# Hybrid decoder block: the mixers' low weight parts, head halves and attention sums made by DMAs in place of vector instructions

## The chip, the cores and the metric

The kernel runs on one NeuronCore of a Trainium2 chip. The metric is the device time of one execution in microseconds, given as the median of several runs. A core has a matrix engine (TensorE, PE in the profile, with its weight loads as PEld), a vector engine (VectorE, DVE), an activation engine (ScalarE, ACT), a general engine (GpSimd, POOL) and a queue engine (SyncE, SP). Each runs its own list of instructions strictly in order; semaphores hold an instruction back until what it needs is there, and everything behind it on that engine waits too. DMAs are issued from SP (the "hardware" queue of the profile) and from POOL (the "software" queue); a DMA that adds to its destination is issued from POOL here.

## The reference

One layer of a hybrid trunk on 1024 tokens of width 1024, all in float32. What matters for the change is attention group B; the rest is cut.

```python
hn = rms_norm(h, norm1_g[i]);  proj = hn @ w_in[i]
a_b, a_c, a_h, q, k, v, c_u, c_v = jnp.split(proj, split_idx, axis=-1)
y_a = a_b * short_conv(a_c * a_h, conv_w[i])                 # width 256
q = rms_norm(q.reshape(bsz, s_len, 8, 64), q_norm_g[i]);  k = ...  # per head
# stick breaking, 8 heads of 64, strictly causal:
z = einsum(q, k) / 8
weights = where(causal, exp(log_sigmoid(z) + suffix_sum(log_sigmoid(-z))), 0)
y_b = einsum(weights, v)
y_c = spatial_gating(gelu(c_u), gelu(c_v), ...)              # width 256
h = h + concat([y_a, y_b, y_c]) @ w_out
f = square(relu(rms_norm(h, norm2_g) @ w_ff1));  h = h + f @ w_ff2
h = h + sigmoid(rms_norm(h, norm3_g) @ w_ple_gate) * (p @ w_ple_proj)
```

## The kernel before, in words

Nearly every product is made of three matmuls on numbers that are split into a rounded high part and a low remainder (`hi`, `lo`; float32r): hi·hi, hi·lo and lo·hi (`product`, L157). A split is two instructions: ACT writes `hi` (a rounding copy), then DVE, or POOL where `low` says so, writes `lo = x - hi` (`split`, L131). A weight tile comes by a DMA on SP into one of 7 staging buffers (`stage`, L64) and is split into two of 20 buffers of the pool `wp` (`load_w`, L141). The staging buffer is free again when `lo` is made; a pair of `wp` buffers is free when its last matmul has run.

Stages: loads and gating MLP (to about 80 us), then projection of the first pair of heads; then from about 105 to 412 us the attention of the four pairs of heads, each woven by `weave` (L262) with filling work for PE: the projection of the next pair (`project`, L306), and for the last pair the convolution's projections (`convolve`, L559); then `w_out`, the MLP (a Strassen-like scheme, 570 to 1172 us) and the gate.

`project(pr)` loads eight weight tiles of 128x384, one for each block of 128 input channels (`wk`, k = 0 to 7). For each of eight token blocks t it runs 24 matmuls (8 k times 3) into one of two PSUM banks, normalizes queries and keys (ACT square, DVE sums, POOL `rs` = power -1/2, DVE `qk`), and splits the values `V`. Every second t, `turn_qk` transposes `qk` on PE and splits it. Each token half (th = 0 for t = 0 to 3, th = 1 for t = 4 to 7) has tiles of 128x512 per head hh: `QS[hh]` stacks the high and the low part of the query on the two halves of the partitions, `KH[hh]` holds the key's high part twice, `KL[hh]` its low part once and zeros. Before, KL is written by two DVE instructions on 64 rows each (L370), the halves are brought to their places by three ACT copies (L374 to L376) and three DVE copies (L377 to L379) of 64x512.

`attend(pr)` goes through eight steps (head 0 with g = 0 to 3, then head 1 with g = 3 to 0; g is a block of 256 queries). `stick` makes `z` on PE, two sigmoids on ACT (`rem`, `wt`), a running product on DVE (L413), and a multiplication on POOL or DVE (L416). `gather` transposes the weights on PE (`w_tr`), splits them (ACT `wT_hi`, DVE `wT_lo`) and multiplies by V into `av`, whose two halves of partitions hold V's high and low contribution. Before, ACT copies the lower half out (L462) and DVE adds the upper (L463) into `y_b`, which goes to DRAM on SP.

Between the steps, `block_sums` (L282) issues DMAs on POOL that work on the MLP's second weight in DRAM (`w_sums`): at most two per call, of 1 MB each, plain (L300) or accumulating (L297), placed behind POOL's last multiplication of the step. The order on each engine is not that of the code alone: a scheduler places each instruction by a simulated timeline. A DMA on POOL also waits for the one eight DMAs earlier on that queue to have landed, and a DMA on SP likewise.

Of the kernel before, what the change touches and what calls it, by code (L numbers as in the profile page):

```python
# [32 lines left out]
def hybrid_block(ctx: ExitStack, tc: tile.TileContext, a: dict):  # L33
# [27 lines left out]
    def slot(s, dt=F32, shape=(P, HT)):  # L61
        return sp.tile(list(shape), dt, tag="slot", name=name(s))
# [10 lines left out]
    def halves(s, dt=F32, shape=(P, HT)):  # L73
        return [slot(s, dt, shape) for _ in range(2)]
# [4 lines left out]
    def half_tmp(s, dt=F32):  # L79
        return tp.tile([P, 256], dt, tag="half", name=name(s), bufs=3)  # L80
# [50 lines left out]
    def split(src, hi, lo, scale=None, low=nc.vector):  # L131

        if scale is None:
            nc.scalar.copy(hi, src)  # L134
            low.tensor_tensor(out=lo, in0=src, in1=hi, op=ALU.subtract)  # L135
        else:
            nc.scalar.activation(hi, src, AF.Copy, scale=scale)
            nc.vector.scalar_tensor_tensor(out=lo, in0=src, scalar=scale, in1=hi,  # L138
                                           op0=ALU.mult, op1=ALU.subtract)

    def load_w(src, cols, low=nc.vector):  # L141

        st = stage(src, cols)
        hi = wp.tile([P, 384], F32R, tag="w", name=name("whi"))
        lo = wp.tile([P, 384], F32R, tag="w", name=name("wlo"))
        split(st, hi[:, :cols], lo[:, :cols], low=low)
        return hi, lo

    def load_units(src):
# [155 lines left out]

    def project(pr):  # L306

        wk = [load_w(a["w_qkv"][pr, k], 384, nc.gpsimd if pr and k % 2 == 0 else nc.vector)
              for k in range(KT)]

        QS = [[None, None], [None, None]]

        KH = [[None, None], [None, None]]
        KL = [[None, None], [None, None]]
        V = [None] * 4
        low_q = [None, None]
        heads[pr] = QS, KH, KL, V, low_q
        for t in range(KT):
            th, ts = block(t)
            if t % 4 == 0:  # L320
                for hh, other in enumerate((hi_p, lo_p)):
                    KL[hh][th] = slot("KL", F32R)
                    nc.gpsimd.memset(KL[hh][th][other].bitcast(F32), 0.0)
                KH[0][th] = slot("KH", F32R)
                QS[0][th] = slot("QS", F32R)
                low_q[th] = slot("q_lo", F32R)
                QS[1][th] = slot("QS", F32R)
# [17 lines left out]
            nc.vector.tensor_tensor(  # L345
                out=qk[:, t % 2].rearrange("p (h d) -> p h d", d=HD),
                in0=ps[:, :256].rearrange("p (h d) -> p h d", d=HD),
                in1=rs.unsqueeze(2).broadcast_to([P, 4, HD]), op=ALU.mult)
            if t % 2 == 0:
                V[t // 2] = slot("V", F32R, (P, 2, 2, 2, HD))  # L350
            v = V[t // 2][:, t % 2]
            split(ps[:, 256:].rearrange("p (h d) -> p h d", d=HD), v[:, :, 0], v[:, :, 1], scale=r1[t])
            if t % 2 == 1:
                later(72, lambda t=t, qk=qk: turn_qk(heads[pr], t, qk))

    def turn_qk(head, t, qk):

        QS, KH, KL, _, low_q = head
        th = t // 4
        tr = bank(ps_tr, "qk_tr")  # L360
        for i in range(2):
            for j in range(2):
                o = j * 256 + i * P
                nc.tensor.transpose(tr[:, o:o + P], qk[:, i, j * P:(j + 1) * P], ident)
# [3 lines left out]
        nc.scalar.activation(KH[0][th][:, ws], tr[:, 256:], AF.Copy, scale=gk)  # L368
        for hh, own in enumerate((lo_p, hi_p)):
            nc.vector.scalar_tensor_tensor(out=KL[hh][th][own, ws], in0=tr[own, 256:],  # L370
                                           scalar=gk[own], in1=KH[0][th][own, ws],
                                           op0=ALU.mult, op1=ALU.subtract)
        if t % 4 == 3:
            nc.scalar.copy(KH[1][th][hi_p], KH[0][th][hi_p])  # L374
            nc.scalar.copy(KH[1][th][lo_p], KH[0][th][hi_p])
            nc.scalar.copy(KH[0][th][hi_p], KH[0][th][lo_p])  # L376
            nc.vector.tensor_copy(QS[1][th][hi_p], QS[0][th][hi_p])  # L377
            nc.vector.tensor_copy(QS[1][th][lo_p], low_q[th][hi_p])
            nc.vector.tensor_copy(QS[0][th][hi_p], low_q[th][lo_p])  # L379
        return 8  # L380

    PROJECT = KT * 72 + 32

    def attend(pr):

        QS, KH, KL, V, _ = heads[pr]
        yb = halves("y_b")
        weights = {}

        def stick(hh, g):  # L390
# [32 lines left out]
        def gather(hh, g):  # L423
# [21 lines left out]
            for j in range(-2, g + 1):  # L445
# [6 lines left out]
                for kb, o, first in parts:  # L452
                    m = 256 - first * P
                    lhs = V[kb // 2][:, kb % 2, hh].rearrange("p two d -> p (two d)")
                    for part in (hi, lo):
# [2 lines left out]
                                         stop=kb == 2 * g + 1 and part is lo)  # L458
                yield 8

            low = half_tmp("av_lo")
            nc.scalar.copy(low[:HD], av[HD:])  # L462
            nc.vector.tensor_tensor(out=yb[g // 2][own, (g % 2) * 256:(g % 2 + 1) * 256],  # L463
                                    in0=av[:HD], in1=low[:HD], op=ALU.add)
            if hh == 1 and g % 2 == 0:
                nc.sync.dma_start(y_dram[pr, g // 2], yb[g // 2])

        steps = [(0, g) for g in range(4)] + [(1, g) for g in reversed(range(4))]
        yield from stick(*steps[0])
# [127 lines left out]
    for h in range(2):  # L597
        for k in range(2):
            st = stage(a["pT"][k * P:(k + 1) * P, half[h]])
            if h == 0:  # L600
                wple.append([load_w(a["w_ple_proj"][k * P:(k + 1) * P, :384], 384)])
            p_parts[k][h] = pair("p")
            split(st, *p_parts[k][h])
    for c0, n in UNITS[1:]:
        for k in range(2):
            wple[k].append(load_w(a["w_ple_proj"][k * P:(k + 1) * P, c0 * P:(c0 + n) * P], n * P))
    vu_parts = []
    first_half = normalize(0)
    for n in range(KT):
# [475 lines left out]
```

## Time and profile before

| what | value |
|---|---|
| time, median of 3 runs | 1270.49 us (1269.83 to 1271.85) |
| the profiled execution's own time | 1269.84 us |
| its span | 1268.1 us |
| mean granted TensorE clock | 0.981 |
| PE / DVE / ACT / POOL busy | 1212.7 / 879.3 / 604.4 / 363.9 us |
| DMA packets, bytes | 118699, 234.89 MB |

A row of the profile's groups reads: line, engine, operation, out<-in, shapes, count | busy time, mean of one in ns | idle time of that engine just before, and what ended it. The view of windows gives, for each stretch of the span, the busy time of each engine with its number of instructions, and the granted clock of TensorE (1.00 is full speed). The view of waits names who waited for whom, with total, number and longest in us. Rows of DMA issues give count, size and the median time from issue to landing.

### The profile page before, as it was taken

The numbers are of one execution on the slowest core, as the hardware profiler recorded it, in microseconds if no ns is written. First come the engines' busy times: TensorE is split into PE (matmuls) and PEld (weight loads), VectorE is DVE, ScalarE is ACT, GpSimd is POOL, SyncE is SP. The second block draws the span as 40 slices with busy tenths as digits, with TensorE's granted clock in tenths as the row PEclk, the third lists the DMA queues.
The fourth block names the chain that finished last, engine by engine and source line by source line (L and its number), as shares of the span: only waits on it lengthen the run. The fifth ranks groups of instructions, "written<-read, shape, count | busy, mean of one in ns | idle before, by whom it ended". The sixth has DMA issues, their size and how long they took to land.

```text
span 1268.1 us, 17511 instructions
## 1 busy us (share of the span) xinstructions
PE 1212.7 (96%) x5868; PEld 1033.1 (81%) x5868; DVE 879.3 (69%) x1324; ACT 604.4 (48%) x1167; POOL 363.9 (29%) x365
## 2 busy tenths in 40 slices
PE   9999898899999898959999999999999999999998
PEld 7898798888888787748888888888888888888887
DVE  7746887898879654666877867777756465686443
ACT  7625655666566354553343333345644354555211
POOL 2324443465222212233543443431000000122110
PEclk9998998999999999979999999999999999999999
DMA  9503157788541287789999999858956565553231
GB/s 321 196 18 132 68 166 231 168 193 159 119 98 34 95 274 195 197 227 214 260 255 258 238 248 260 241 183 308 359 179 224 187 211 183 192 174 101 78 113 50
DMA packets 118699, 234.89 MB, mean 185 GB/s; under 512 B 13104, under 2 KB 20528, under 8 KB 118352
## 3 DMA queue, kind: packets, MB, share of 16 engines
q1 hardware_dynamic: 94752, 168.08, 39.5%
q0 software_dynamic: 23856, 65.70, 23.1%
q8 instruction: 46, 0.75, 0.3%
q14 instruction: 45, 0.37, 0.1%
HBM read 176.57 MB, written 78.64 MB: 201 GB/s over the span
## 4 chain that ended last, share of the span: by engine, by line
PE 82%; DVE 8%; DMA 5%; issue 2%; ACT 1%; POOL 0%; SPq 0%; DVEq 0%; POOLq 0%; ACTq 0%
PE d_ps L731 24%; PE f_ps L731 23%; PE qkv_ps L161 3%; PE qkv_ps L162 3%; PE qkv_ps L163 3%; PE g_ps L161 2%; PE g_ps L163 2%; PE g_ps L162 2%; DVE rem L413 2%; PE av L456 2%; DMA h_dram<-h 1%; PE w_tr L438 1%; PE cv_ps L161 1%; PE cv_ps L163 1%; PE cv_ps L162 1%
## 5 line engine op out<-in xcount | busy, mean ns | idle before, releaser
L135 DVE TENSOR_TENSOR w_lo<-raw,w_hi 128x512 fp32r<-128x512 f32 x268 | 238.9, 894 | 97.2 <-ACT w_hi L134 92.7
L134 ACT CAST w_hi<-raw 128x512 fp32r<-128x512 f32 x268 | 164.8, 619 | 246.1 <-PE d_ps L731 118.1
L731 PE MATMUL f_ps<-hn_hi,w_hi 128*128 128x512 f32 x448 | 176.4, 394 | 11.1 <-ACT v L872 11.1
L731 PE MATMUL f_ps<-hn_lo,w_hi 128*128 128x512 f32 x448 | 175.5, 392 | 0.0
L731 PE MATMUL f_ps<-hn_hi,w_lo 128*128 128x512 f32 x448 | 175.1, 391 | 0.0
L731 PE MATMUL d_ps<-f_hi,w_hi 128*128 128x512 f32 x448 | 174.3, 389 | 0.0
L731 PE MATMUL d_ps<-f_lo,w_hi 128*128 128x512 f32 x448 | 174.3, 389 | 0.0
L731 PE MATMUL d_ps<-f_hi,w_lo 128*128 128x512 f32 x448 | 174.3, 389 | 0.0
L731 PEld LDWEIGHTS f_ps<-hn_hi,w_hi 128*128 128x128 f32 x448 | 84.9, 190 | 29.5 <-ACT v L872 11.5
L719 POOL TENSOR_TENSOR S<-S,sq 128x512 f32<-128x512 f32 x14 | 22.2, 1588 | 274.3 <-ACT sq L785 274.3
L731 PEld LDWEIGHTS f_ps<-hn_lo,w_hi 128*128 128x128 f32 x448 | 84.8, 189 | 18.2 <-issue 0.5
L731 PEld LDWEIGHTS f_ps<-hn_hi,w_lo 128*128 128x128 f32 x448 | 84.8, 189 | 17.7
L731 PEld LDWEIGHTS d_ps<-f_hi,w_hi 128*128 128x128 f32 x448 | 84.1, 188 | 17.6
L731 PEld LDWEIGHTS d_ps<-f_hi,w_lo 128*128 128x128 f32 x448 | 84.1, 188 | 17.5
L731 PEld LDWEIGHTS d_ps<-f_lo,w_hi 128*128 128x128 f32 x448 | 84.1, 188 | 17.3
L413 DVE TENSOR_TENSOR_SCAN rem<-rem 128x128 f32<-128x128 f32 (+3 forms) x64 | 88.9, 1392 | 10.3 <-ACT rem L409 9.7
L161 PE MATMUL qkv_ps<-whi,xn_hi 128*128 128x384 f32 x256 | 91.8, 359 | 2.5 <-DVE V L138 2.5
L163 PE MATMUL qkv_ps<-whi,xn_lo 128*128 128x384 f32 x256 | 89.7, 351 | 0.0
L162 PE MATMUL qkv_ps<-wlo,xn_hi 128*128 128x384 f32 x256 | 89.4, 349 | 0.0
L135 DVE TENSOR_TENSOR f_lo<-raw,f_hi 128x512 fp32r<-128x512 f32 x112 | 77.5, 723 | 3.9 <-ACT f_hi L134 3.7
L416 POOL TENSOR_TENSOR wt<-wt,rem 128x127 f32<-128x127 f32 (+4 forms) x40 | 44.3, 1109 | 106.8 <-DVE rem L413 44.0
L134 ACT CAST f_hi<-raw 128x512 fp32r<-128x512 f32 x112 | 67.0, 620 | 16.2 <-DMA raw<-f_dram 12.1
(213 smaller groups left out, 2663.4 us busy)
## 6 DMA issues: line engine op xcount, KB each, us to landing
raw<-in_w_ff SPq DMA_DIRECT2D x160, 256.0 KB, 3.8
raw<-f_dram SPq DMA_DIRECT2D x112, 256.0 KB, 4.7
raw<-w_sums SPq DMA_DIRECT2D x64, 256.0 KB, 3.7
f_dram<-f SPq DMA_DIRECT2D x48, 256.0 KB, 4.2
f_dram<-t SPq DMA_DIRECT2D x48, 256.0 KB, 4.0
w_sums<-in_w_ff POOLq DMA_DIRECT2D x8, 1024.0 KB, 11.7
w_sums<-w_sums POOLq DMA_DIRECT2D x8, 1024.0 KB, 12.6
raw<-in_w_ff POOLq DMA_DIRECT2D x32, 256.0 KB, 5.2
```

The lines of the kernel that those rows point to most:

```text
L134: nc.scalar.copy(hi, src)
L135: low.tensor_tensor(out=lo, in0=src, in1=hi, op=ALU.subtract)
L161: nc.tensor.matmul(ps, lh, rh, start=first and i == 0, stop=False)
L162: nc.tensor.matmul(ps, lh, rl, start=False, stop=False)
L163: nc.tensor.matmul(ps, ll, rh, start=False, stop=last and i == len(terms) - 1)
L413: nc.vector.tensor_tensor_scan(out=back, data0=back, data1=back, initial=1.0, op0=ALU.mult, op1=ALU.bypass)
L416: done = (nc.vector if on_vector else nc.gpsimd).tensor_tensor(out=wt[:, :W - 1], in0=wt[:, :W - 1], in1=rem[:, 1:W], op=ALU.mult)
L438: nc.tensor.transpose(tr[:, n:n + P], wts[i][:, kb * P:(kb + 1) * P], ident)
L456: nc.tensor.matmul(av[:, first * P:], lhs, part[:, o:o + m], start=kb == 0 and part is hi, stop=kb == 2 * g + 1 and part is lo)
L719: return eng.tensor_tensor(out=out, in0=x, in1=y, op=ALU.add)
L731: nc.tensor.matmul(bank, l, r, start=first and k == 0 and i == 0, stop=k == len(b) - 1 and i == 2, skip_group_check=True)
```

## The change

Three edits, all in the mixers. (1) `load_w`, for the projections of `project` and `convolve` (50 tiles): ACT writes minus the rounded weight into `lo`, then `hi`; a DMA on POOL adds the weight itself to `lo`. The subtraction on DVE or POOL goes. The six tiles of `w_ple_proj` keep the old way. (2) `turn_qk`: the key's low part is made for all 128 rows by one DVE instruction into a tile of its own, `k_lo`; at the end of each token half eight DMAs of 64x512 on SP bring the halves of QS, KH and KL to their places. The six copies and one of two L370 go. The last two of the eight overwrite rows that earlier ones read, and so wait for those to have landed. (3) `gather`: ACT copies all 128 rows of `av` into a tile `av_sb` of one token half; after its second part an accumulating DMA on POOL adds the lower rows to the upper, and a DMA on SP stores 64 rows to DRAM (16 of each kind in place of 8 stores). ACT's copy of 64 rows and DVE's addition go.

```diff
-    def load_w(src, cols, low=nc.vector):
+    def load_w(src, cols, by_dma=True):
         st = stage(src, cols)
         hi = wp.tile([P, 384], F32R, tag="w", name=name("whi"))
         lo = wp.tile([P, 384], F32R, tag="w", name=name("wlo"))
-        split(st, hi[:, :cols], lo[:, :cols], low=low)
+        if by_dma:
+            nc.scalar.activation(lo[:, :cols], st, AF.Copy, scale=-1.0)
+            nc.scalar.copy(hi[:, :cols], st)
+            nc.gpsimd.dma_start(lo[:, :cols], st, accum_op=ALU.add)
+        else:
+            split(st, hi[:, :cols], lo[:, :cols])
         return hi, lo
...
-        wk = [load_w(a["w_qkv"][pr, k], 384, nc.gpsimd if pr and k % 2 == 0 else nc.vector)
-              for k in range(KT)]
+        wk = [load_w(a["w_qkv"][pr, k], 384) for k in range(KT)]
...
         split(tr[:, :256], QS[0][th][:, ws], low_q[th][:, ws], scale=gq)
-        nc.scalar.activation(KH[0][th][:, ws], tr[:, 256:], AF.Copy, scale=gk)
-        for hh, own in enumerate((lo_p, hi_p)):
-            nc.vector.scalar_tensor_tensor(out=KL[hh][th][own, ws], in0=tr[own, 256:],
-                                           scalar=gk[own], in1=KH[0][th][own, ws],
-                                           op0=ALU.mult, op1=ALU.subtract)
+        split(tr[:, 256:], KH[0][th][:, ws], low_k[th][:, ws], scale=gk)
         if t % 4 == 3:
-            nc.scalar.copy(KH[1][th][hi_p], KH[0][th][hi_p])
-            nc.scalar.copy(KH[1][th][lo_p], KH[0][th][hi_p])
-            nc.scalar.copy(KH[0][th][hi_p], KH[0][th][lo_p])
-            nc.vector.tensor_copy(QS[1][th][hi_p], QS[0][th][hi_p])
-            nc.vector.tensor_copy(QS[1][th][lo_p], low_q[th][hi_p])
-            nc.vector.tensor_copy(QS[0][th][hi_p], low_q[th][lo_p])
+            for to, src, rows, of in (
+                    (KH[1], KH[0], lo_p, hi_p), (KH[1], KH[0], hi_p, hi_p),
+                    (QS[1], QS[0], hi_p, hi_p), (QS[1], low_q, lo_p, hi_p),
+                    (KL[0], low_k, lo_p, lo_p), (KL[1], low_k, hi_p, hi_p),
+                    (KH[0], KH[0], hi_p, lo_p), (QS[0], low_q, hi_p, lo_p)):
+                nc.sync.dma_start(to[th][rows].bitcast(F32), src[th][of].bitcast(F32))
...
-            low = half_tmp("av_lo")
-            nc.scalar.copy(low[:HD], av[HD:])
-            nc.vector.tensor_tensor(out=yb[g // 2][own, (g % 2) * 256:(g % 2 + 1) * 256],
-                                    in0=av[:HD], in1=low[:HD], op=ALU.add)
-            if hh == 1 and g % 2 == 0:
-                nc.sync.dma_start(y_dram[pr, g // 2], yb[g // 2])
+            th = g // 2
+            first = (hh, th) not in sums
+            if first:
+                sums[hh, th] = slot("av_sb")
+            y = sums[hh, th]
+            nc.scalar.copy(y[:, (g % 2) * 256:(g % 2 + 1) * 256], av)
+            if not first:
+                nc.gpsimd.dma_start(y[:HD], y[HD:], accum_op=ALU.add)
+                nc.sync.dma_start(y_dram[pr, th][own], y[:HD])
+                del sums[hh, th]
```

The scheduler orders the mixers anew. Three places show it, all at the end of the second pair's attention, where the fourth pair's weights come in. Numbers in names are tile numbers and differ between the two programs: wt_3046 before is wt_3061 after, wlo_3167 is the low part of the last weight tile (k = 7) of the fourth pair, wlo_4044 and wlo_4051 belong to the convolution.

POOL before, around the four accumulating `w_sums` DMAs of that place:

```order
L416 TENSOR_TENSOR wt_3046<-wt_3046,rem_3045 128x255
L297 DMA w_sums<-in_w_ff 512x512 x2
L297 DMA w_sums<-w_sums 512x512 x2
L135 TENSOR_TENSOR wlo_3115<-stage_3112,whi_3114 128x384
L323 MEMSET KL_3148 64x512
L323 MEMSET KL_3150 64x512
L135 TENSOR_TENSOR wlo_3127<-stage_3124,whi_3126 128x384
L135 TENSOR_TENSOR wlo_3139<-stage_3136,whi_3138 128x384
L416 TENSOR_TENSOR wt_3214<-wt_3214,rem_3213 128x127
```

POOL after, at the same place (the last row is the accumulating DMA of the attention's sums of the second pair, head 1):

```order
L418 TENSOR_TENSOR wt_3051<-wt_3051,rem_3050 128x127
L150 DMA wlo_3160<-stage_3157 128x384
L418 TENSOR_TENSOR wt_3061<-wt_3061,rem_3060 128x255
L303 DMA w_sums<-in_w_ff 512x512 x2
L303 DMA w_sums<-w_sums 512x512 x2
L150 DMA wlo_3167<-stage_3164 128x384
L150 DMA wlo_4044<-stage_4041 128x384
L150 DMA wlo_4051<-stage_4048 128x384
L175 TENSOR_TENSOR rs_3110<-ss_3107,mhalf 128x4
L470 DMA av_sb_2939<-av_sb_2939 64x512
```

The weights' low parts were instructions of POOL and DVE; now three of them, and a sum, are DMAs that stand behind four 1 MB DMAs on the same queue. One pair earlier the same stands once: wt_2154, two accumulating `w_sums` DMAs, then wlo_2259 (the third pair's k = 4), av_sb_2032, wlo_2266.

SP after, a little later; each load waits for its staging buffer (stage_4445 for wlo_3167's DMA, stage_4452 for wlo_4044's), each store for its accumulating DMA, and the next two rows are the last joins for the third pair's second token half:

```order
L66 DMA stage_4445<-in_w_conv 128x384
L66 DMA stage_4452<-in_w_conv 128x384
L471 DMA y_dram<-av_sb_2939 64x512
L471 DMA y_dram<-av_sb_3192 64x512
L381 DMA KH_2703<-KH_2703 64x512
L381 DMA QS_2704<-q_lo_2705 64x512
```

Before, there were no joins on SP; its queue held loads and eight stores of `y_b` alone.

PE after, where these are used (z_3327 is the third pair's first score of t = 4, head 0):

```order
L168 MATMUL qkv_ps_3181<-wlo_3167,xn_hi_426 128x384
L169 MATMUL qkv_ps_3181<-whi_3166,xn_lo_427 128x384
L168 MATMUL qkv_ps_3298<-wlo_3167,xn_hi_426 128x384
L169 MATMUL qkv_ps_3298<-whi_3166,xn_lo_427 128x384
L458 MATMUL av_87<-wT_hi_3309,V_2402 128x256
L458 MATMUL av_87<-wT_lo_3310,V_2402 128x256
L458 MATMUL av_87<-wT_hi_3309,V_2402 128x128
L458 MATMUL av_87<-wT_lo_3310,V_2402 128x128
L404 MATMUL z_3327<-KH_2703,QS_2704 128x128
```

The scheduler has moved the k = 7 products of the first two token blocks (qkv_ps_3181, qkv_ps_3298) behind the rest of both; before, they stood with the others of their block, in the order of k. Both PSUM banks of the projection stay taken until they have run.

More of the change, by code (lines that the diff above doesn't have):

```diff
@@ L315, in project @@
         V = [None] * 4
-        low_q = [None, None]
-        heads[pr] = QS, KH, KL, V, low_q
+        low_q, low_k = [None, None], [None, None]
+        heads[pr] = QS, KH, KL, V, low_q, low_k
         for t in range(KT):
@@ L326, in project @@
                 low_q[th] = slot("q_lo", F32R)
+                low_k[th] = slot("k_lo", F32R)
                 QS[1][th] = slot("QS", F32R)
@@ L356, in turn_qk @@
     def turn_qk(head, t, qk):
-        QS, KH, KL, _, low_q = head
+        QS, KH, KL, _, low_q, low_k = head
         th = t // 4
@@ L384, in attend @@
     def attend(pr):
-        QS, KH, KL, V, _ = heads[pr]
-        yb = halves("y_b")
+        QS, KH, KL, V, *_ = heads[pr]
+        sums = {}
         weights = {}
@@ L600, in hybrid_block @@
             if h == 0:
-                wple.append([load_w(a["w_ple_proj"][k * P:(k + 1) * P, :384], 384)])
+                wple.append([load_w(a["w_ple_proj"][k * P:(k + 1) * P, :384], 384, False)])
             p_parts[k][h] = pair("p")
@@ L605, in hybrid_block @@
         for k in range(2):
-            wple[k].append(load_w(a["w_ple_proj"][k * P:(k + 1) * P, c0 * P:(c0 + n) * P], n * P))
+            wple[k].append(load_w(a["w_ple_proj"][k * P:(k + 1) * P, c0 * P:(c0 + n) * P], n * P, False))
     vu_parts = []
```

## The prediction

> **What bounds the kernel now.** I read the page first, then windows, then the waits of one stage.
>
> ```profile
> span 1268.1 us, 17511 instructions
> ...
> PE 1212.7 (96%) x5868; PEld 1033.1 (81%) x5868; DVE 879.3 (69%) x1324; ACT 604.4 (48%) x1167; POOL 363.9 (29%) x365
> ```
>
> PE is busy for 96% of the span, so an edit gains only where PE is idle or slow. The change touches the mixers; the windows cut at the starts of the pairs' attention (the first two numbers are the stretch and PE's busy time, then PEld, DVE, ACT, POOL, the granted clock and the DMA share).
>
> ```profile
> 112.00:190.00 78.00, 68.63 (x409) 64.60 (x409) 62.41 (x104) 46.49 (x111) 37.32 (x38) 0.93 0.44 141
> 190.00:268.00 78.00, 70.38 (x429) 66.37 (x429) 63.52 (x107) 48.31 (x118) 36.64 (x40) 0.93 0.69 191
> 268.00:340.00 72.00, 65.63 (x429) 61.86 (x429) 64.72 (x109) 48.04 (x116) 31.43 (x29) 1.00 0.77 152
> 340.00:442.00 102.00, 98.18 (x530) 83.11 (x529) 78.94 (x113) 52.98 (x115) 28.75 (x24) 1.00 0.34 83
> 442.00:460.00 18.00, 16.90 (x63) 13.75 (x64) 9.32 (x15) 8.67 (x16) 2.10 (x3) 0.81 0.84 282
> ```
>
> In the first four PE is idle for 9.4, 7.6, 6.4 and 3.8 us, 27 us in all. The clock of 0.93 in two windows of 78 us costs at most another 11 us. So 38 us is all that the mixers can give. DVE is busy for 269.6 of these 330 us (82%), and it is DVE that PE waits for, as the waits of PE from 90 to 435 us say (total us, times, longest):
>
> ```profile
> PE qk_tr L364 <- DVE qk L345: 5.5, 4, 2.7
> PE av L456 <- DVE wT_lo L135: 4.0, 4, 1.7
> PE w_tr L438 <- DVE wt L416: 3.1, 3, 1.4
> PE w_tr L438 <- DVE KL L370: 2.8, 2, 1.4
> PE av L456 <- DVE y_b L463: 2.7, 4, 1.3
> PE qkv_ps L161 <- DVE V L138: 2.5, 3, 0.8
> PE w_tr L438 <- DVE wT_lo L135: 2.2, 1, 2.2
> ```
>
> These are 22.8 us. No row names a DMA: weights reach PE through DVE in time.
>
> **The change part by part: what leaves.** The groups of the same stretch:
>
> ```profile
> L135 DVE TENSOR_TENSOR wlo<-stage,whi 128x384 fp32r<-128x384 f32 (+1 forms) x29 | 20.2, 708 | 6.9 <-ACT whi L134 6.8
> L134 ACT CAST whi<-stage 128x384 fp32r<-128x384 f32 (+1 forms) x40 | 18.9, 502 | 12.2 <-DMA stage<-in_w_qkv 6.1 <-PE cv_ps L162 5.0 <-DMA stage<-in_w_conv 0.8
> L370 DVE SCALAR_TENSOR_TENSOR KL<-qk_tr,c_gk,KH 64x256 fp32r<-64x256 f32 x32 | 15.3, 478 | 2.5 <-ACT KH L368 2.2
> L135 POOL TENSOR_TENSOR wlo<-stage,whi 128x384 fp32r<-128x384 f32 x11 | 13.3, 1219 | 0.6 <-ACT whi L134 0.6
> L463 DVE TENSOR_TENSOR y_b<-av,av_lo 64x256 f32<-64x256 f32 x32 | 13.2, 411 | 3.4 <-ACT av_lo L462 2.9
> ...
> L376 ACT CAST KH<-KH 64x512 fp32r<-64x512 f32 x8 | 5.0, 619 | 1.8 <-DVE KL L370 1.6
> ...
> L377 DVE CAST QS<-QS 64x512 fp32r<-64x512 f32 x8 | 3.8, 476 | 0.0
> ```
>
> DVE loses 20.2 (low parts) + half of 15.3 (one KL in place of two) + 13.2 (y_b) + 24 copies at up to 0.476 (11.4) = 52 us, some 18% of its work here. ACT loses 24 copies of 0.619 (14.9) and gains 50 negations of 0.502 (25), ten of them before the stretch: about +5 us on an engine with a third of its time free. POOL loses 13.3.
>
> What this is worth to PE: the waits for KL and y_b go whole (5.5 us). The other 17.3 wait for instructions that stay, but that stand behind fewer others on DVE. The lower end is that none of it goes, as each is also a step of a chain through ACT and POOL, the upper that all goes, and the 11 us of clock too. I take half, 9 us, because DVE was fuller than PE's fill could hide in just the windows with the idle time. The gain is 15 us (5.5 to 38).
>
> **What comes: DMAs on two queues.** The prices of one accumulating DMA of 256 KB that POOL issues (engine time in ns as minimum, median, maximum, then its landing), and of a plain one on SP:
>
> ```profile
> L747 POOL DMA_DIRECT2D raw<-in_w_ff x32: 863/876/1357, 494.9 to 811.3; - x32
> ```
> ```profile
> S<-sq POOLq DMA_DIRECT2D x14, 256.0 KB, 5.1
> ...
> y_dram<-y_c SPq DMA_DIRECT2D x4, 256.0 KB, 2.2
> ```
>
> 66 DMAs on POOL at 0.88 us are 58 us of engine time, 9 of them before the stretch: net +36 us on 134 busy of 330, which alone leaves POOL half idle. A low part now comes about 5 us after ACT instead of 0.7. Eight weight tiles have ten places, so tiles k = 2 to 7 of a pair can be filled only when the last token block of the pair before has let go of the buffers; from there PE has about 24 matmuls of its own and the woven attention ahead, at 70.38/429 = 0.164 us a matmul at least 4 us, so an undisturbed DMA is late by about 1 us, less than the 2.7 us gap before qk_tr at the first such place. I price that place at nothing either way.
>
> What is not undisturbed is the software queue. This is the time to landing where four accumulating DMAs of 1 MB were issued one behind the other (from 264 to 300 us), then where two were (300 to 303 us), and the second of these two alone:
>
> ```profile
> w_sums<-in_w_ff POOLq DMA_DIRECT2D x2, 1024.0 KB, 13.7
> w_sums<-w_sums POOLq DMA_DIRECT2D x2, 1024.0 KB, 26.3
> ```
> ```profile
> w_sums<-in_w_ff POOLq DMA_DIRECT2D x2, 1024.0 KB, 10.6
> ```
> ```profile
> w_sums<-in_w_ff POOLq DMA_DIRECT2D x1, 1024.0 KB, 12.8
> ```
>
> Issued within 2 us, the second pair landed 12.6 us after the first: the queue serves them in order, at 6.3 us per MB beside other loads, and at 12.8 + 0.7 - 8.4 = 5.1 where little else ran (8.4 is the first of that pair, 2 x 10.6 - 12.8; 0.7 the estimated distance of the two issues, half of the 1.4 us between 265.01 and 266.37 below). A small DMA behind them waits for all. Before, none was waited for soon; after, wlo_3167 stands right behind these four.
>
> ```profile
> 264.43 0.64 POOL L416 TENSOR_TENSOR wt<-wt,rem 128x255 f32<-128x255 f32 x1
> 265.01 2.18 POOL L297 DMA_DIRECT2D w_sums<-in_w_ff  x2
> 266.37 2.90 POOL L297 DMA_DIRECT2D w_sums<-w_sums  x2
> ```
> ```profile
> 284.50 0.31 PE L402 MATMUL z<-KH,QS 128*128 128x128 f32 x1
> ```
>
> Let T be the end of that multiplication, 265.1. Before, PE was through the two token blocks' products and started the score of t = 4 at 284.5, T + 19.4. After, that score (z_3327) needs KH_2703, whose DMA stands on SP behind two stores, and these wait for POOL's DMAs behind the four: three low parts and two sums, 0.84 MB. Loaded as before, the fourth lands at 266.7 + 26.3 + 3.2 = T + 31, the 0.84 MB 5.3 later, store issue and join 2.5 more: T + 39. With the lighter rate: T + 0.6 + 8.4 + 3 x 5.1 = T + 24.3, + 4.3 + 2.5 = T + 31. So PE is 12 to 19 us late here. Waiting in between does not help it, since the projection's two banks are held by the missing k = 7. I take 14, nearer to the lower end, because the convolution's loads that shared the engines (seven or more before) are fewer.
>
> One pair earlier wlo_2259 lands behind two such DMAs: 0.7 + 12.8 + 1.0 = 14.5 us after the first's issue. PE reaches its use 38 matmuls after the one that consumes wt_2154, 6 us at 0.164: a stall of 0 (if PE runs behind, as it did before) to 8.5 us. I take 5.
>
> The TensorE clock: windows with gaps show 0.93. The Trainium skill, "TensorE: Matmul & The Clock Gate", section "What's actually happening", says that the array falls to half rate after an idle window of about 3.4 us; a stall of 14 us would by that add about 1.7 us, an estimate from that page. I count gaps that go and gaps that come as equal: 0 (-5 to +5).
>
> Joins and the end of the attention: six joins of 2.2 and two that wait for them cost some 5 us against 2 before, hidden where a half is needed tens of us later. At the end, the last store waits for an accumulate:
>
> ```profile
> 430.62 1.97 DMA y_dram<-y_b
> 433.62 4.89 DMA stage<-in_w_out
> ```
>
> The store starts about 4 us later, but only the fourth of the eight terms of the first output block needs it. Together +1 (-3 to +6).
>
> Sum: -15 + 14 + 5 + 0 + 1 = +5 us on the profiled execution's 1269.84. The median of the runs shown, 1270.49, is 0.65 above it: 1275.5 us.
>
> **The rivals.** (a) *The low parts arrive in time; DVE's relief shows* (faster). Decided at one point: whether wlo_3167 and the join behind it land before T + 19. For it: DVE leads every wait above, and PE may reach these places late, as at the earlier one. Against it: the 26.3 us row. Both stalls go, 1270.5 - 15 = 1255. The Trainium skill, "DMA: Bandwidth & Descriptors", section "Anatomy of one DMA — SWDGE (gpsimd) path", fits 2.0 us plus bytes at 436 GB/s for a DMA of this queue: by that an estimate of 2 + 4 x 2.4 = 12 us for the four, which is this rival's result; the rows (10.6 for the pair's median, 26.3 for the last two) disagree for accumulating DMAs, so it gets no more than its own chance. (b) *They cancel* (no change): only the 5.5 us of KL and y_b are gained, as the rest are chains, and one stall of 5 or 6 us appears: 1270.5. For it: ACT and POOL steps stand in every chain. (c) *SP becomes a bound* (slower by more): stage loads wait for low-part DMAs and block joins at every change of pair, not just the one priced: 14 us a second time, 1289. Against it: only one of the four places has four DMAs ahead.
>
> **How the numbers follow.** What a measurement of this kernel can tell from no change is about 0.2%, 2.5 us. Forecast (stalls outweigh the relief by 3 to 15 us) 0.37, (c) 0.10, (b) 0.16, (a) 0.37. Slower is 0.47, the same 0.16, faster 0.37. The signs hold most of the chance on both sides; the forecast's own range is 1273 to 1286. The whole range reaches from (a) at 1254 to the costs' upper bounds with the gain's lower: -5.5 + 19 + 8.5 + 1 = +23, 1293.
>
> **What would show it.** In the profile after: DVE in the four windows near 220 us; no wait for KL or y_b; a gap on PE of 8 us or more that a DMA ends, before qkv_ps L168 (on wlo) or z L404 (on KH), about 15 to 30 us after the four `w_sums` DMAs; a landing above 15 us among the `wlo` DMAs. The forecast is wrong if PE has no wait for a DMA above 3 us there, or if its waits for DVE do not fall by 10 us or more.

## The result, and the profile after

The kernel after takes 1308.62 us (median of 4 runs, 1304.82 to 1313.41) against 1270.16 of the kernel before beside it: a ratio of 1.031 (95% interval 1.0275 to 1.0345), slower by 38 us. The prediction had the sign, and 5 us of the 38; its range ended at 1293. The profiled execution's span grew from 1268.1 to 1304.5 us. Of the runs below, one of e12 (1563.46 us, at a mean granted clock of 0.74) is left out of that kernel's figures.

The page of the kernel after: DVE has lost 43 us, and PE is busy 6 us longer for the same 5868 matmuls.

```profile
span 1304.5 us, 17713 instructions
...
PE 1218.7 (93%) x5868; PEld 1038.4 (80%) x5868; DVE 836.5 (64%) x1214; ACT 606.6 (46%) x1193; POOL 398.6 (31%) x419
```

Its windows, cut at nearly the same work as those of before (columns as there: PE, PEld, DVE, ACT, POOL, granted clock, DMA share):

```profile
112.00:189.00 77.00, 65.49 (x409) 61.46 (x408) 53.72 (x81) 47.59 (x116) 37.10 (x43) 0.98 0.65 187
189.00:278.00 89.00, 72.25 (x421) 66.80 (x421) 53.12 (x82) 47.12 (x116) 41.51 (x47) 0.88 0.90 227
278.00:370.00 92.00, 70.25 (x430) 67.56 (x429) 52.45 (x83) 47.60 (x118) 40.41 (x44) 0.85 0.81 159
370.00:480.00 110.00, 102.66 (x547) 87.49 (x546) 65.90 (x84) 51.94 (x123) 44.67 (x42) 0.97 0.50 101
```

The first window is as short as before; the next three are 11, 20 and 8 us longer, for much the same number of matmuls. PE's idle time in the four is 11.5, 16.8, 21.8 and 7.3, 57 us against 27. DVE is busy for 225 us in place of 270, and the clock is at 0.88 and 0.85 where it was 0.93 and 1.00. PE's waits from 90 to 480 us (total, times, longest):

```profile
PE qkv_ps L168 <- DMA wlo<-stage: 19.1, 3, 14.5
PE z L404 <- DMA QS<-q_lo: 13.2, 3, 7.3
PE w_tr L440 <- DVE wT_lo L135: 6.1, 2, 4.8
PE av L458 <- DVE wT_lo L135: 4.5, 4, 1.7
PE z L404 <- ACT wt L412: 3.8, 4, 2.9
PE w_tr L440 <- DVE wt L418: 3.2, 3, 1.7
PE qkv_ps L167 <- DVE V L138: 2.8, 2, 2.4
PE av L458 <- ACT av_sb L468: 2.4, 3, 1.6
PE qk_tr L370 <- DVE qk L351: 1.6, 1, 1.6
```

32.3 us are waits for DMAs, where before no row named one. The waits for DVE are 18.2 us (24.1 before: the 22.8 of the seven rows in the prediction and 1.3 in two smaller ones), those for ACT and POOL 6.7 (6.2 in the two rows of ACT, 0.5 in one of POOL; 0.3 before).

The place that the prediction priced, at the third change of pair (the start of the third pair's attention): time to landing of the DMAs issued from 280 to 284.2 us, then PE's two longest waits behind them and the end of SP's queue (in brackets the idle time before, and what ended it).

```profile
w_sums<-in_w_ff POOLq DMA_DIRECT2D x2, 1024.0 KB, 15.1
w_sums<-w_sums POOLq DMA_DIRECT2D x2, 1024.0 KB, 26.0
wlo<-stage POOLq DMA_DIRECT2D x3, 192.0 KB, 28.6
```
```profile
312.09 0.69 PE L168 MATMUL qkv_ps<-wlo,xn_hi 128*128 128x384 f32 x1 [14.51 <-DMA wlo<-stage]
319.32 0.45 PE L404 MATMUL z<-KH,QS 128*128 128x128 f32 x1 [4.84 <-DMA QS<-q_lo]
```
```profile
312.06 1.63 SPq L66 DMA_DIRECT2D stage<-in_w_conv  x2
315.07 1.11 SPq L471 DMA_DIRECT2D y_dram<-av_sb  x2
316.23 0.59 SPq L381 DMA_DIRECT2D KH<-KH  x1
316.91 0.55 SPq L381 DMA_DIRECT2D QS<-q_lo  x1
```

A low part of 192 KB needs 28.6 us here, longer than the 1 MB DMAs ahead of it; the two issued just before the four landed after 4.1 and 4.8 us. When it has landed PE goes on (312), SP can load into the buffer (312), then store the sums (315), then issue the last joins (316), and PE's next score waits for these. At the fourth change of pair two 1 MB DMAs stand ahead of a sum, whose store on SP holds the joins until 393.9 us:

```profile
402.66 0.44 PE L404 MATMUL z<-KH,QS 128*128 128x128 f32 x1 [7.34 <-DMA QS<-q_lo]
```

### The profile page after: what moved, and what is told of

It is laid out like the page before. It is cut to its first block, busy times and chain, and to the rows that moved or that the text cites. A ratio compares the mean times of both kernels' runs of the same rounds, so it can differ in the third digit from the quotient of the medians.

```text
span 1304.5 us, 17713 instructions
## 1 busy us (share of the span) xinstructions
PE 1218.7 (93%) x5868; PEld 1038.4 (80%) x5868; DVE 836.5 (64%) x1214; ACT 606.6 (46%) x1193; POOL 398.6 (31%) x419
## 4 chain that ended last, share of the span: by engine, by line
PE 78%; DMA 11%; DVE 4%; issue 2%; ACT 2%; POOL 1%; SPq 0%; DVEq 0%; POOLq 0%; ACTq 0%
PE d_ps L737 23%; PE f_ps L737 23%; DMA wlo<-stage 4%; PE qkv_ps L168 3%; PE qkv_ps L167 3%; PE qkv_ps L169 2%; PE g_ps L167 2%; PE g_ps L169 2%; PE g_ps L168 2%; PE av L458 2%; PE w_tr L440 2%; DMA av_sb<-av_sb 1%; DVE rem L415 1%; DMA h_dram<-h 1%; PE vu_ps L169 1%
## 5 line engine op out<-in xcount | busy, mean ns | idle before, releaser
L135 DVE TENSOR_TENSOR w_lo<-raw,w_hi 128x512 fp32r<-128x512 f32 x268 | 241.8, 905 | 99.3 <-ACT w_hi L134 95.3
L415 DVE TENSOR_TENSOR_SCAN rem<-rem 128x128 f32<-128x128 f32 (+3 forms) x64 | 92.3, 1443 | 35.3 <-ACT rem L411 35.0
L737 PEld LDWEIGHTS f_ps<-hn_lo,w_hi 128*128 128x128 f32 x448 | 84.8, 189 | 18.2 <-issue 0.5
L418 POOL TENSOR_TENSOR wt<-wt,rem 128x127 f32<-128x127 f32 (+4 forms) x40 | 48.4, 1392 | 73.4 <-DVE rem L415 58.7
```

The source lines that it names most:

```text
L415: nc.vector.tensor_tensor_scan(out=back, data0=back, data1=back, initial=1.0, op0=ALU.mult, op1=ALU.bypass)
L418: done = (nc.vector if on_vector else nc.gpsimd).tensor_tensor(out=wt[:, :W - 1], in0=wt[:, :W - 1], in1=rem[:, 1:W], op=ALU.mult)
L737: nc.tensor.matmul(bank, l, r, start=first and k == 0 and i == 0, stop=k == len(b) - 1 and i == 2, skip_group_check=True)
```

## The experiments

Each was timed in 3 rounds beside the kernel before, whose medians in the five sets were 1267.87, 1268.66, 1269.86, 1267.87 and 1267.91 us. The first set asks whether the loss is the queue behind the 1 MB DMAs, or something that each edit does by itself.

**after_nosums and before_nosums.** The same edit on both kernels; where the MLP reads sums it reads blocks of `w_ff2`.

```diff
-            block_sums(8 * pr + i, last_pool[0])
...
-        s = w_sums[int(of[1]) - 1].rearrange("r n -> (r n)")
+        s = a["w_ff2"][int(of[1]) - 1].rearrange("c j p n -> (c j p n)")
```

> The kernel after, with the w_sums DMAs of the mixers left out; the MLP reads blocks of w_ff2 of the same size in place of the sums, so the products of that stage are other numbers with the same work. To be compared with the kernel before with the same thing left out. Queue theory (the 36 us lost are small DMAs, low parts and sums and the joins behind their stores, that stand behind 1 MB DMAs): PE's waits for DMAs in the mixers, 32.3 us in the kernel after, fall to under 6, the mean granted clock comes back to 0.98, and the time is within 8 us of the kernel before without its w_sums, on either side. Chain theory (a low part by DMA comes some 5 us late and POOL's 30 us of extra work delay everything, whatever else the queue holds): at least 15 us above the kernel before without w_sums, PE still waiting 15 us or more for wlo or joins.

> The kernel before with the w_sums DMAs of the mixers left out, the MLP reading blocks of w_ff2 in their place (other numbers, same work). Both theories: nothing waits soon for a w_sums DMA in the kernel before, so it gains little: 1262 to 1271 us, the most of it from POOL's 30 us of issues that stand before multiplications. Below 1258 would mean that these DMAs already cost the kernel before by what they take from others, and the comparison with the kernel after must take that into account.

Measured: 1259.01 (0.9934, 0.9916 to 0.9953) and 1249.71 us (0.9866, 0.9844 to 0.9888). So the w_sums DMAs cost the kernel before 18.2 us, which neither theory expected (1262 or more) and no wait of PE names, and the kernel after 49.6. The 31.4 us between these are the size of PE's 32.3 us of waits for DMAs, and without w_sums not one such wait is left (PE's longest, after_nosums, 90 to 440 us):

```profile
PE qkv_ps L167 <- DVE V L138: 6.4, 3, 2.4
PE av L458 <- DVE wT_lo L135: 6.0, 5, 1.7
PE w_tr L440 <- DVE wt L418: 4.7, 6, 1.8
```

The queue theory holds for 31 of some 40 us, but what stays without these DMAs is just over the 8 us that it allowed: 9.3 us, in waits for DVE (22 us against 14 in before_nosums) and in PE's busy time (1208.3 us against 1204.2).

**e1_low, e2_joins, e3_sums and e23.** Edits alone, and 2 with 3. Against the kernel after, an edit is undone by the lines of the kernel before:

```diff
 # without edit 1 (e2_joins, e3_sums, e23)
-            nc.gpsimd.dma_start(lo[:, :cols], st, accum_op=ALU.add)
...
+        split(st, hi[:, :cols], lo[:, :cols], low=low)
...
 # without edit 2 (e1_low, e3_sums)
-                nc.sync.dma_start(to[th][rows].bitcast(F32), src[th][of].bitcast(F32))
+            nc.scalar.copy(KH[1][th][hi_p], KH[0][th][hi_p])
...
 # without edit 3 (e1_low, e2_joins)
-                nc.gpsimd.dma_start(y[:HD], y[HD:], accum_op=ALU.add)
...
+                                    in0=av[:HD], in1=low[:HD], op=ALU.add)
```

> The kernel before with edit 1 alone: weights' low parts by accumulating DMAs, with the old copies and additions. Queue theory: the low part behind the w_sums DMAs stalls PE once or twice, 10 to 18 us in all, with the clock after it: 1280 to 1295 us. Chain theory: the loss is spread over the pairs, with many waits of 1 to 3 us: 1290 us or more. If the joins are the larger part of the loss (third view), 1275 us or less, PE waiting under 6 us for wlo.

> The kernel after with edit 1 undone: low parts of the weights on DVE and POOL as before, joins and sums by DMAs. Queue theory: no low part stands behind a 1 MB DMA, but the accumulating sums of the attention do, and the joins stand behind their stores on SP: PE waits 3 to 13 us for joins, 1270 to 1285 us. Third view (joins are the larger part): 1285 us or more. If DVE's relief by edits 2 and 3 is worth what the waits for KL and y_b were and the joins are hidden: 1262 to 1267 us.

> The kernel before with edit 2 alone: k_lo by one instruction and eight joins by DMAs on SP; the attention's sums stay on ACT and DVE, the weights' low parts on DVE and POOL. Edits 2 and 3 together cost 19 us, with one wait of 9.6 us for a join that stood behind the stores of sums that stood behind w_sums DMAs. Queue theory: without the accumulating sums no store on SP waits for POOL's queue, so no join is late: waits for joins under 3 us, 1268 to 1277 us (what is left over is the order of DVE's work, waits of PE for wT_lo behind a long running product). Joins are late by themselves: a wait above 5 us for QS or KH again, 1280 us or more.

> The kernel before with edit 3 alone: the attention's halves added by accumulating DMAs behind the w_sums DMAs on POOL's queue, stored by SP; no joins. Queue theory: the late stores hold only loads on SP that are needed tens of us later, so PE waits for no DMA above 2 us; ACT's and DVE's relief are small: 1262 to 1272 us. If the accumulating sums themselves cost (POOL's issue before multiplications, or SP's loads behind stores that wait): 1275 us or more.

Measured: e1_low 1294.85 us (1.0212, 1.0196 to 1.0228), e23 1286.82 (1.016, 1.0133 to 1.0188), e2_joins 1273.37 (1.0031, 1.0009 to 1.0054), e3_sums 1258.97 (0.9919, 0.9894 to 0.9945). Edit 3 alone is a gain of 9.7 us, more than expected, edit 2 costs 5, within the queue theory's range, and edit 1 27. The times of e1_low and e23 decide little: 1294.85 lies in the ranges of both the queue and the chain theory, and 1286.82 just above the queue theory's, where the third view begins (1285), though PE's waits for joins (11.7 us in all) are of the size that the queue theory gave. The mechanism expected of e1_low is a miss: PE waits 4.5 us for low parts, not 10 to 18. There the queue shows in a third way, on POOL itself:

```profile
289.58 2.63 POOL L150 DMA_DIRECT2D wlo<-stage  x3
292.94 0.86 POOL L150 DMA_DIRECT2D wlo<-stage  x1 [0.73 <-ACT wt L415]
298.63 0.86 POOL L150 DMA_DIRECT2D wlo<-stage  x1 [4.83 <-issue]
304.52 0.86 POOL L150 DMA_DIRECT2D wlo<-stage  x1 [5.03 <-issue]
305.08 0.73 POOL L421 TENSOR_TENSOR wt<-wt,rem 128x127 f32<-128x127 f32 x1
```

The last three issues here start about 0.5 us after a w_sums DMA eight places ahead has landed (292.42, 298.12 and 304.00): the program's limit of eight under way holds POOL, a multiplication stands behind, and PE waits 11.2 us for it. In e23 the largest wait is one of 9.6 us for QS, behind stores of sums.

**n1_low and n23.** Edit 1 alone, and edits 2 and 3, with the w_sums DMAs left out (the diffs above put together).

> Edit 1 alone, and the w_sums DMAs of the mixers left out (the MLP reads blocks of w_ff2 in their place: other numbers, same work). Without them the whole change stood 9.3 us above the kernel before. View 1, POOL's issues delay the multiplications and norms behind them: edit 1, with most of the issues, has most of the 9: 1255 to 1261 us against 1249.7. View 2, it is the order on DVE (second parts of V and wT_lo put behind running products of 1024 that take 3.2 in place of 2.3 us): edit 1 costs under 3 us, 1247 to 1253.

> Edits 2 and 3 without edit 1, and the w_sums DMAs of the mixers left out (other numbers in the MLP, same work). View 1 (POOL's issues): under 3 us above the kernel before without w_sums, 1247 to 1253. View 2 (DVE's order): most of the 9.3 us, 1254 to 1261, with PE's waits for wT_lo and V longer than before and none for a join above 2 us.

Measured: n1_low 1267.7 us (0.9991, 0.9973 to 1.0008), n23 1254.98 (0.9877, 0.9836 to 0.9919): 18.0 and 5.3 above before_nosums, where the whole change is 9.3 above. So edit 1 does the most, as view 1 has it, but by more than view 1 gave (1261 at most), n23 lies in view 2's range, at its edge (1254), and the parts do not add up; PE waits 2.0 us for low parts in n1_low. The orders of the three differ, and neither view holds for both.

**e12 and e13.** Edits 1 and 2, and 1 and 3 (the lines above, undone for edit 3 and edit 2).

> Edits 1 and 2, the attention's sums as before (ACT and DVE). Alone edit 1 cost 27 us, edit 2 5, edit 3 gained 9.5, edits 2 and 3 together cost 19. Queue theory: the joins are late only where stores on SP wait for accumulating sums behind w_sums DMAs; without the sums only stage loads that wait for low parts can hold them: waits for joins under 6 us, low parts late as in edit 1, 1290 to 1302 us. If the joins are late in the same way without edit 3 (waits of 10 us or more): 1305 us or more.

> Edits 1 and 3, the heads' halves copied by ACT and DVE as before. Queue theory: low parts behind w_sums DMAs stall PE as with edit 1 alone, the late stores hold nothing that is needed: near the sum of the two alone, 1268 + 27 - 9.5, so 1278 to 1293 us, with no wait for KH or QS. If edit 3 adds a cost with edit 1 as it does with edit 2 (some 24 us there): 1300 us or more.

Measured: e12 1317.7 us (1.0415, 1.0358 to 1.0473), e13 1290.92 (1.0177, 1.0146 to 1.0208). e12 goes against the queue theory as it stood and with the other case that was named: it is slower than the whole change, and the joins are nearly as late without any sum on the queue:

```profile
PE qkv_ps L168 <- DMA wlo<-stage: 21.3, 3, 10.1
PE z L404 <- DMA QS<-q_lo: 10.1, 2, 6.4
```

So it takes no late sum ahead of them: SP's loads, which wait for low parts to free their buffers, are enough (at the fourth change a low part lands 16.6 us after its issue, the load starts 0.03 us later, the joins behind it). e13 came out as expected in sum, but its largest wait is POOL's again (16.1 us for `wt`), 10.1 for low parts and none for a join. Edit 3 gains 9 us or more beside edits 1 and 2, perhaps 4 beside edit 1 (the two intervals overlap), and costs 13 beside edit 2 alone.

**after_spread, before_spread, e3_spread, e23_spread.** The same 32 DMAs, two in each of steps 2 to 5 of every pair:

```diff
+    TURNS = {}
+    A1, A2, A3 = PASSES[:3]
+    for n, (piece, todo) in enumerate([(p, x) for p in range(4) for x in (A1, A2, A3)]):
+        TURNS[n] = [(piece, x) for x in todo]
...
+        pr, step = divmod(i, 8)
+        if not 2 <= step < 6:
+            return
...
-            for to, what in PASSES[i % 4]:
+            for piece, (to, what) in TURNS[4 * pr + step - 2]:
```

> The kernel after with the same 32 w_sums DMAs, but issued only in steps 2 to 5 of each pair's attention, so that none stands at a change of pair, where the weights of the next pair come in. Queue theory: what made the w_sums DMAs cost 49.6 us in the kernel after against 18.2 before was their place ahead of low parts, sums and joins that were needed soon; moved, PE's waits for DMAs fall from 32 to under 10 us and the time to 1270 to 1285 us. If it is their load (DMA engines, POOL's issues) and not their place, the time stays above 1295 us.

> The kernel before with edit 3 alone (1259.0 us measured) and the 32 w_sums DMAs moved to steps 2 to 5 of each pair's attention. Queue theory: the sums of the attention end in each step and stand behind w_sums DMAs in either place, with nobody waiting soon: within 6 us of e3_sums, 1253 to 1265. If the place of the w_sums DMAs costs by itself also without small DMAs that are waited for, as the 18 us of the kernel before may be, it becomes faster: 1245 to 1253.

> The kernel before with the 32 w_sums DMAs moved to steps 2 to 5 of each pair. If the place at the changes of pair costs any kernel, as edit 3 alone suggests (12.1 us faster when moved): 1253 to 1261. If the place matters only where small DMAs stand on the same queue: 1265 to 1272.

> Edits 2 and 3 with the w_sums DMAs moved to steps 2 to 5 of each pair. Edits 2 and 3 cost 19 us at the old place and 5.3 us without these DMAs. Queue theory: moved, no join waits behind a 1 MB DMA: PE's waits for joins under 3 us, 1250 to 1260, still above edit 3 alone moved (1246.9). If the joins are hidden and DVE's relief shows: 1238 to 1246.

Measured: after_spread 1277.06 us (1.0058, 1.0029 to 1.0087), before_spread 1260.44 (0.9928, 0.9893 to 0.9963), e3_spread 1246.85 (0.9835, 0.9803 to 0.9867), e23_spread 1253.95 (0.9883, 0.9854 to 0.9912). In after_spread the waits for DMAs are down to 5.1 us:

```profile
PE z L411 <- DMA QS<-q_lo: 2.8, 1, 2.8
PE qkv_ps L168 <- DMA wlo<-stage: 2.3, 4, 0.8
```

Most of it was the place: moving took 31.6 of the 49.6 us off the kernel after, and 7 to 9 of the 18.2 off the kernel before. The rest, 18.0 and some 10 us, stays with these DMAs wherever they stand. e3_spread, edit 3 alone with these DMAs moved, is 1.65% faster than the kernel before; adding edit 2 to it costs 6 to 7 us, without a wait for a join among PE's rows.

**free and free_nosums, free_pool and free_joins.** What is the relief worth when no new DMA takes its place, and which new DMAs cost when no 1 MB DMA is there? `free` leaves out the low parts' and sums' DMAs and the joining itself (the two heads share QS, KH and k_lo); free_pool keeps POOL's DMAs, free_joins the joins. All but `free` are without the w_sums DMAs, and with the joining go the memsets of KL.

```diff
 # left out in free, free_nosums and free_joins
-            nc.gpsimd.dma_start(lo[:, :cols], st, accum_op=ALU.add)
...
-                nc.gpsimd.dma_start(y[:HD], y[HD:], accum_op=ALU.add)
...
 # changed in free, free_nosums and free_pool
-                nc.sync.dma_start(to[th][rows].bitcast(F32), src[th][of].bitcast(F32))
...
+                KH[0][th] = KH[1][th] = slot("KH", F32R)
+                QS[0][th] = QS[1][th] = slot("QS", F32R)
...
+                low_k[th] = KL[0][th] = KL[1][th] = slot("k_lo", F32R)
```

> The kernel after with every DMA that the three edits add left out, and nothing in their place: a weight's low part stays minus the weight, the attention's halves are not added (the upper rows are stored alone), the two heads share one QS, one KH and k_lo, and the memsets of KL go; the output is other numbers. What is left of the change is DVE's and POOL's relief and ACT's 5 us. Load theory (the prediction's gain term): 15 us below the kernel before, 1250 to 1260, or more. Order theory (PE waits for DVE because of what stands ahead in the order, not because DVE is full): within 6 us of the kernel before, 1263 to 1275, PE's waits for DVE not under 12 us.

> The same without the w_sums DMAs of the mixers. The kernel before without them took 1249.7 us, the one after 1259.0. Load theory: 1230 to 1242. Order theory: 1245 to 1256; then the new DMAs themselves cost the rest up to 1259.0 where no 1 MB DMA is ahead.

> The kernel after without w_sums DMAs and without the joins (the two heads share QS, KH and k_lo, no memsets; other numbers): of the new DMAs only the low parts' and the sums' on POOL are left. If POOL's accumulating DMAs cost the 29 us (issues of 0.9 us and more before multiplications, low parts 3 to 6 us later): 1250 to 1259. If the joins do: 1229 to 1236.

> The kernel after without w_sums DMAs and without the accumulating DMAs on POOL (low parts stay minus the weight, the attention's halves are not added; other numbers): of the new DMAs only the 64 joins on SP are left, with their tiles and the memsets of KL. If the joins cost the 29 us (scores of a new token half start later, so the attention's steps bunch up): 1250 to 1259. If POOL's DMAs do: 1229 to 1236. Both near 1240 to 1248: the two share it.

Measured: free 1232.6 us (0.971, 0.9683 to 0.9738), free_nosums 1229.91 (0.9687, 0.966 to 0.9714), free_pool 1233.36 (0.9725, 0.9707 to 0.9744), free_joins 1251.15 (0.9862, 0.9842 to 0.9882). With nothing in its place the change gains 35 us, so the order theory falls; the w_sums DMAs then cost 2.7, and PE waits for hardly anything (free, 90 to 403 us):

```profile
PE av L445 <- DVE wT_lo L135: 1.8, 3, 0.8
PE av L445 <- ACT av_sb L455: 0.3, 1, 0.3
PE qkv_ps L166 <- DVE V L138: 0.2, 1, 0.2
```

Without w_sums, POOL's 66 DMAs cost 3.5 us, and the joining with its tiles 21.2. PE names no DMA there, so why? Nearly half of it is PE's busy time, 1208.0 us in free_joins and 1198.1 in free_nosums for the same 5868 matmuls (mean granted clock 0.983 and 0.988); the rest is idle time. The projection's instructions (`qkv_ps`) in stretches of 8 us in the middle of the first pair's attention, first in free_joins, then in free_nosums, then in before_nosums (the count after PE's busy time is that of its matmuls):

```profile
136.00:144.00 8.00, 3.64 (x20) 3.19 (x19) 0.82 (x2) 0.38 (x1) 1.00 0.07 16
144.00:152.00 8.00, 0.00 (x0) 0.00 (x0) 0.00 (x0) 0.00 (x0) 1.00 0.01 2
152.00:160.00 8.00, 0.00 (x0) 0.00 (x0) 0.34 (x1) 0.78 (x2) 0.79 0.00 0
```
```profile
136.00:144.00 8.00, 5.66 (x27) 4.42 (x26) 0.00 (x0) 0.41 (x1) 1.00 0.01 2
144.00:152.00 8.00, 4.66 (x25) 4.10 (x24) 1.52 (x4) 1.22 (x3) 1.00 0.00 0
152.00:160.00 8.00, 4.84 (x23) 3.65 (x22) 0.41 (x1) 0.84 (x2) 1.00 0.08 18
```
```profile
136.00:144.00 8.00, 4.68 (x24) 3.63 (x22) 0.42 (x1) 0.00 (x0) 1.00 0.01 2
144.00:152.00 8.00, 0.00 (x0) 0.00 (x0) 0.00 (x0) 0.78 (x2) 1.00 0.00 0
152.00:160.00 8.00, 5.30 (x20) 4.99 (x20) 0.77 (x2) 0.00 (x0) 0.79 0.00 0
```

In free_joins PE has no filling work from 140.3 to 160.5 us, through the longest steps of the attention: the projection stands before its fifth token block. before_nosums has the same hole at the same block, from 141.3 to 153.9; free_nosums has none there. Just ahead of that block the program takes the tiles of the second token half, whose first instruction is the memset of KL; it comes at 145.32 us in before_nosums and at 156.93 in free_joins:

```profile
145.32 1.10 POOL L323 MEMSET KL<- 64x512 f32 x2
```
```profile
156.93 1.09 POOL L327 MEMSET KL<- 64x512 f32 x2
```

The change holds eight tiles per half in place of seven, `free` four, of the same 56. That scarce tiles hold the filling work back is argued from this, not shown: the projection goes on 8.6 us after its first memset in before_nosums and 3.5 after it in free_joins, PE's idle time within the hole is 4.1 and 5.4 us, and tiles and joins were not tried apart.

## Why the prediction was wrong

**What bounds it.** Right in the view, wrong in what was read from it. The 38 us that the mixers could give were real: `free` takes 35. But DVE's load was not by itself what held them: free_joins has 52 us less on DVE than before_nosums (821.2 against 873.2) and is 1.4 us slower. A reading that fits the traces, but is not shown, is that PE had run out of filling work, and DVE was then the next in the chain: of the 28 us that PE is idle in the kernel before from 100 to 480 us, 21 lie in seven stretches of over 4 us in which no matmul of the projection runs, the three longest of 12 to 15 us.

**The gain (forecast 15, bounds 5.5 to 38).** This is the step that failed most. The waits for KL and y_b went, as said; waits for wT_lo, ACT and POOL took their place. All of PE's waits for engines in the mixers were 24.4 us and are 24.9: no gain. Those for DVE fell by 5.9 us, not by the 10 or more without which the prediction called itself wrong. "I take half" had no row behind it, and 5.5 was no lower end. The runs without w_sums DMAs say the same: the prediction had -15 for the relief and +1 for the joins, and the two together, free_joins against before_nosums, give +1.4. Whether the relief is worth little, or the joins and their tiles take it back, is open.

**The stall at the third change of pair (forecast 14, bounds 12 to 19).** Right in its mechanism, with its size at the upper end. The first of the four DMAs was issued at 280.89, which puts T at 281.0; the fourth landed at 311.03, T + 30 (31 by the loaded bound), and the score came at 319.32, T + 38 (39). The two waits are 14.5 and 4.8 us, 19.3 together, which the estimate of fewer loads had argued away. By the fit of the Trainium skill, "DMA: Bandwidth & Descriptors", section "Anatomy of one DMA — SWDGE (gpsimd) path", the estimate for the four was 12 us; 30 were measured, so the fit does not hold for these accumulating DMAs from memory to memory beside other loads.

**The stall one pair earlier (forecast 5, 0 to 8.5).** Right: 4.3 us before qkv_ps, behind two w_sums DMAs, and 0.3 in a second short wait.

**Joins and the end (forecast +1, -3 to +6).** The second step that failed. That the joins are "hidden where a half is needed tens of us later" was said of all four changes of pair, while the prediction's own working showed for one of them that SP's queue makes the joins late. The fourth pair's joins stood behind a late store in the same way: 7.3 us, and 1.0 was lost at the first change, 8.3 in all. With the 4.8 above, joins cost 13.2 us of waits. Rival (c), SP as a bound with a second stall, was this mechanism, priced at 0.10.

**The clock (forecast 0, -5 to +5).** Gaps that go and gaps that come were not equal: PE's busy time grew by 6.0 us, just beyond the bound, with windows at 0.88 and 0.85. The largest piece is behind the third change: the clock granted from 312 to 325.5 us is 0.51, so that of the 8.6 us that PE is busy there about 4 are its price (an estimate from these two numbers), where the prediction had 1.7.

Term by term, forecast and measured: gain -15 and +0.5; third change 14 and 19.3; second change 5 and 4.6; joins 1 and 8.3; clock 0 and 6.0. PE's waits outside the mixers, which the prediction left out, fell by 2.3 (from 25.9 to 23.6). The sum is 36.4, the growth of the span. So the sign is right by the mechanism that was named, the stalls; half of the 31 us that were missed is the gain.

By times without this bookkeeping: relief without any joining and its tiles -19.8 (free_nosums against before_nosums), joins with their tiles +21.2, POOL's DMAs +3.5, the two together +4.4 more, and the w_sums DMAs 31.4 dearer: +40.7, which is 1308.62 - 1267.87 (the kernel before of the first set; 38.5 against the one measured beside the kernel after).

**Open** is how much of the 35 us of `free` is DVE's relief and how much the joining and the tiles that it does not have, and by what the w_sums DMAs cost the kernel before its 18 us. Moving them gives back 7 to 9; the traces of before and before_nosums show only where they cost: PE is busy for 1212.7 against 1204.2 us, and idle for 28.4 against 19.9 from 100 to 480 us.

## What to carry to other kernels

Before a vector instruction becomes a DMA, list what stands ahead of that DMA on its queue at the worst place, and what stands behind every wait that it brings to the queues of loads and stores; here one that lands after 4 to 5 us with none of these ahead took 28.6 behind four large ones. A wait for an engine that is 82% busy need not be that engine's load: look first whether the waiting engine had filling work in that stretch, and what held it. And try the parts alone: one of three edits was a gain of 0.8%, and 1.65% once the large transfers were moved away from the changes of pair (0.7% by the move alone).

## What the runs showed of the hardware

The running product on DVE (128x1024) takes 2.28 us, and up to 3.79 while POOL multiplies. In the kernel after:

```profile
243.23 1.76 POOL L418 TENSOR_TENSOR wt<-wt,rem 128x895 f32<-128x895 f32 x1 [4.29 <-DVE rem L415]
243.35 3.79 DVE L415 TENSOR_TENSOR_SCAN rem<-rem 128x1024 f32<-128x1024 f32 x1
244.94 1.01 POOL L303 DMA_DIRECT2D w_sums<-w_sums  x1
246.00 1.09 POOL L328 MEMSET KL<- 64x512 f32 x2
```
```profile
422.29 2.28 DVE L415 TENSOR_TENSOR_SCAN rem<-rem 128x1024 f32<-128x1024 f32 x1
```

The product is longer by 1.51 us, and overlaps the multiplication for 1.64; the DMA issue and the memsets beside it add nothing. Two more products of this size (at 150.10 and 158.76 us) overlap such a multiplication for 1.1 and 1.0 us and take 3.26 and 3.19; one beside two DMA issues alone (at 337.04) takes 2.29. The Trainium skill, "SBUF — State Buffer", section "Who interferes with whom", says that a DVE instruction with two inputs in SBUF contends with a GpSimd instruction that reads SBUF, and not with one that only writes it. The trace agrees: 1.5 us of 1.6 are lost, and none beside the memsets. The PE wait of 4.8 us for wT_lo in the kernel after stands right behind this product, so an order that puts the two together can cost up to these 1.5 us.
